# A Mamba layer on one core: low weight halves moved to VectorE, squares and first conv taps to ScalarE, group sums to PSUM, and a shorter step-size series

## The chip, the cores and the metric

The kernel runs on one core of one Trainium2 chip. The metric is the device time of one launch in microseconds (us). The engines are TensorE (PE, with its weight loads as PEld), VectorE (DVE), ScalarE (ACT), GpSimd (POOL) and SyncE (SP), which here only issues DMAs.

## The reference, cut to what matters

The whole model is two transformer-like blocks over 256 tokens of width 1024: half-step feed-forward layers, one Mamba-2 mixer, windowed attention, then a mixer of latent attention and RWKV, and a PEER layer. The change touches the Mamba-2 mixer alone:

```
zxbcdt = u @ w_in                                # 1024 -> 5152
z, xbc, dt = split(zxbcdt)                       # 2048, 3072, 32
xbc = silu(depthwise_conv(xbc, 4 taps) + b)      # xs, B, C
dt = softplus(dt + dt_bias)
y = scan(xs, dt, -exp(a_log), B, C) + d_skip * xs
y = y * silu(z)
y = rmsnorm over each of 4 groups of 512 columns
return y @ w_out                                 # 2048 -> 1024
```

With 256 tokens the scan is one chunk: `y = (C Bt * decay * dt) x`, where the decay comes from the running sum of `dt * a`.

## The kernel before, in words

Activations lie transposed: 128 features on the partitions, 256 tokens along the free dimension. Every product of float32 matrices is made of three matmuls in a faster format (`mm3`, lines 151 to 155): each operand is split into a high half, which is a rounded copy, and a low half, which is what the copy lost. Weights come from HBM in blocks of 128 x 1024 (512 KB, eight tiles of 128 x 128); `stream` (line 102) keeps one block ahead. ACT makes the high half of a block (line 93), and DVE or POOL subtracts it from the raw block for the low half (line 99). There are four raw buffers and three pairs of halves. The argument `lo_eng` says who makes the low half: "dve", "pool", or "alt", which takes turns and begins with POOL. In the Mamba layer `w_in` has 40 blocks ("alt", line 419: 20 on POOL, 20 on DVE) and `w_out` has 16 ("pool", line 463).

The layer goes through these stages. First come `dt` and the first column pairs. Then a loop of twelve column pairs (lines 450 to 456) makes B, C and xs: 48 matmuls (`proj2`), then `conv` (line 421), which scales the pair by the token's norm (line 423, DVE), multiplies the first of four taps (line 428, DVE), adds the other three (line 432, DVE, three for each of two columns) and applies silu (line 434, ACT). The tile of a column being convolved has two buffers. From pair n = 10 on, each `conv` also takes six steps of the generator `steps` (line 348). That one turns dt into the decay: a transpose, softplus, a series for its logarithm part (lines 375 to 382), then two sums over tokens by matmul with a triangle (lines 393 to 397), whose result is copied at lines 399 to 401. Line 457 runs what is left of it. Line 459 makes the first of four gate projections (`zproj`: two pairs, silu by ACT).

Then four groups run (line 548), woven with `fill`, which deals out the other three gate projections and the output projection as PE work for the gaps. A `group` (line 512) runs four `pair`s: two matmuls that spread the running sums, four Relu and one Exp on ACT (lines 477 to 479), four products on DVE (lines 483, 484), eight matmuls, two DVE operations (lines 493, 494), and POOL's square and sum (lines 496 to 500). Then the group's norm: `rs_tok` (line 184) sums the squares over the partitions by two matmuls of one column (line 190), nine short DVE operations make a reciprocal root (lines 168 to 176), two matmuls spread it (line 198), and DVE and ACT scale and split the group (lines 531 to 533) for the output projection, which adds up in four PSUM banks.

Each engine works through its own queue in order. When the program is built, a scheduler puts the instructions into these queues, near the order in which Python traces them, but an instruction that it holds ready can move ahead. A tile with one name has a fixed number of buffers; the next use waits until the last reader of the oldest is done.

Of the kernel before, what the change touches and what calls it, by code (L numbers as in the profile page):

```python
# [7 lines left out]
F32 = mybir.dt.float32  # L8
# [4 lines left out]
AF = mybir.ActivationFunctionType  # L13
OP = mybir.AluOpType
# [3 lines left out]
T = 256  # L18
KD = 8
EPS = 1e-6  # L20
# [17 lines left out]
def run(*gens):  # L38

    live = [g if isinstance(g, tuple) else (g, 1) for g in gens]  # L40
    while live:
        for x in list(live):
            for _ in range(x[1]):
                if next(x[0], live) is live:
                    live.remove(x)
                    break
# [275 lines left out]
def mamba(K, h, P, w_dt, w_in, w_out, pool):  # L322


    nc = K.nc
    V, A, TE = nc.vector, nc.scalar, nc.tensor
    ident = K.ident
    xhi, xlo, scale = K.norm_in(h, P["ssm_norm"])
# [19 lines left out]
    def steps():  # L348

        small = lambda name: pool.tile([128, 2, 32], F32, name=name)  # L350
        na = pool.tile([128, 32], F32, name="na")
        df = pool.tile([32, T], F32, name="df")
        e, s, s2 = small("sp_e"), small("sp_s"), small("sp_s2")
        A.activation(na, P["alog"], AF.Exp)
        A.activation(df, pdt[:32, :T], AF.Copy)
        yield
        ps = K.bank()
        for st in range(2):
            TE.transpose(ps[:, st * 32:(st + 1) * 32], df[:, st * 128:(st + 1) * 128], ident[:32, :32])
        yield  # L360
        for st in range(2):
            V.scalar_tensor_tensor(dtv[:, st], ps[:, st * 32:(st + 1) * 32], rt[:, st], P["dtb"], OP.mult, OP.add)
        yield
        V.scalar_tensor_tensor(e, dtv, -1.0, dtv, OP.mult, OP.min)
        A.activation(e, e, AF.Exp)
        yield
        V.tensor_scalar(s, e, 2.0, None, OP.add)
        yield
        V.reciprocal(s, s)
        yield  # L370
        V.tensor_mul(s, s, e)
        yield
        V.tensor_mul(s2, s, s)
        yield
        V.tensor_scalar(e, s2, 2.0 / 17, 2.0 / 15, OP.mult, OP.add)
        for c in (13, 11, 9, 7, 5, 3, 1):
            yield
            V.tensor_mul(e, e, s2)
            yield
            V.tensor_scalar(e, e, 2.0 / c, None, OP.add)  # L380
        yield
        V.tensor_mul(e, e, s)
        yield
        V.scalar_tensor_tensor(dtv, dtv, 0.0, e, OP.max, OP.add)
        yield
        V.scalar_tensor_tensor(s, dtv, -1.0, na.unsqueeze(1).to_broadcast([128, 2, 32]), OP.mult, OP.mult)
        yield
        ps = K.bank()
        pf = ps[:32, T:2 * T]
        for st in range(2):  # L390
            o, f = ps[:, st * 32:(st + 1) * 32], pf[:, st * 128:(st + 1) * 128]
            if st:
                TE.matmul(o, K.ones, s[:, 0], start=True, stop=False)
            TE.matmul(o, K.triu, s[:, st], start=st == 0, stop=True)
            if st:
                TE.matmul(f, s[:, 0], K.ones, start=True, stop=False)
            TE.matmul(f, s[:, st], K.triu, start=st == 0, stop=True)
        yield
        V.tensor_copy(acum, ps[:, 0:64].rearrange("p (a b) -> p a b", a=2))
        V.tensor_copy(ahl[0:32], pf)  # L400
        V.tensor_sub(ahl[32:64], pf, ahl[0:32].bitcast(F32))
# [14 lines left out]
                TE.transpose(ps[:, i * 128:(i + 1) * 128], xs[:, 4 * g + i, st * 128:(st + 1) * 128], ident)  # L416
            A.activation(xtok[:, st, g * 512:(g + 1) * 512], ps, AF.Copy)

    blk_x = K.stream(w_in, lo_eng="alt")

    def conv(n, pr):
        xp = xps[n // 2 % 2]
        V.tensor_tensor(xp[:, :, 3:], pr, rs2, OP.mult)
        w = P["convw"]
        for j in range(2):
            c = (n + j + 16) % 24
            y = pool.tile([128, T], F32, name="cv", tag="cv", bufs=2)
            V.tensor_scalar(y, xp[:, j, 0:T], w[:, c, 0:1], None, OP.mult)
            for q in range(1, 4):
                if n >= 10:  # L430
                    next(st, None)
                V.scalar_tensor_tensor(y, xp[:, j, q:q + T], w[:, c, q:q + 1], y, OP.mult, OP.add)
            dst = BC[:, n + j] if n < 8 else xs[:, n + j - 8]
            A.activation(dst, y, AF.Silu, bias=P["convb"][:, c:c + 1])

    def zproj(g):
        for m in range(2):
            o = []
            yield from K.proj2_steps(blk_x, 8 * (24 + 4 * g + 2 * m), xhi, xlo, o)
            V.tensor_tensor(zs[:, 4 * g + 2 * m:4 * g + 2 * m + 2], o[0], rs2, OP.mult)  # L440
        A.activation(zs[:, 4 * g:4 * g + 4], zs[:, 4 * g:4 * g + 4], AF.Silu)
        zdone.append(g)
# [4 lines left out]
    rs, rt = scale(lambda: up(2))  # L447
    rs2 = rs.unsqueeze(1).to_broadcast([128, 2, T])
    st = steps()
    for n in range(0, 24, 2):  # L450
        conv(n, first[n // 2] if n < 4 else K.proj2(blk_x, 8 * n, xhi, xlo))
# [2 lines left out]
                cb(g)  # L454
        if n > 12 and n % 4 == 0:
            tok((n - 16) // 4)
    run(st)
    zdone = []
    run(zproj(0))
    tok(2)  # L460
    tok(3)
    acc = [K.bank("wo") for _ in range(4)]
    blk = K.stream(w_out, lo_eng="pool")
    todo = []

    def pair(g, pr, yv, sq):

        i = g * 4 + pr
        ps = K.bank()
        sc = pool.tile([128, 2, 384], F32, name="sc", tag="sc", bufs=4)  # L470
        for e in range(2):
            hd = 2 * i + e
            TE.matmul(ps[:, e * T:(e + 1) * T], K.identr[:, hd:hd + 1].to_broadcast([64, 128]), ahl, start=True, stop=True)
        yield
        for e in range(2):
            hd = 2 * i + e
            A.activation(sc[:, e, 0:256], ps[:, e * T:e * T + 256], AF.Relu, bias=adt[:, 0, hd:hd + 1], scale=-1.0)
            A.activation(sc[:, e, 256:384], ps[:, e * T + 128:e * T + 256], AF.Relu, bias=adt[:, 1, hd:hd + 1], scale=-1.0)
        A.activation(sc, sc, AF.Exp, scale=-1.0)
        yield  # L480
        for e in range(2):
            hd = 2 * i + e
            V.scalar_tensor_tensor(sc[:, e, 0:256], sc[:, e, 0:256], adt[:, 0, 32 + hd:33 + hd], cbT[:, g, 0:256], OP.mult, OP.mult)
            V.scalar_tensor_tensor(sc[:, e, 256:384], sc[:, e, 256:384], adt[:, 1, 32 + hd:33 + hd], cbT[:, g, 256:384], OP.mult, OP.mult)
        yield
        py = K.bank()
        for e in range(2):
            hd = 2 * i + e
            o = py[64 * e:64 * e + 64]
            TE.matmul(o[:, 0:256], xtok[:, 0, hd * 64:hd * 64 + 64], sc[:, e, 0:256], start=True, stop=False)  # L490
            TE.matmul(o[:, 128:256], xtok[:, 1, hd * 64:hd * 64 + 64], sc[:, e, 256:384], start=False, stop=True)
        yield
        V.scalar_tensor_tensor(yv, xs[:, i], P["dskip"][:, i:i + 1], py[:, :T], OP.mult, OP.add)
        V.tensor_mul(yv, yv, zs[:, i])
        if pr == 0:
            nc.gpsimd.tensor_mul(sq, yv, yv)
        else:
            s1 = K.tmp.tile([128, T], F32, name="sq", tag="sq", bufs=2)
            nc.gpsimd.tensor_mul(s1, yv, yv)
            nc.gpsimd.tensor_add(sq, sq, s1)  # L500

    def w_out_blocks(g, yhi, ylo):
        for n in range(KD):
# [7 lines left out]

    def group(g):
        yv = pool.tile([128, 4, T], F32, name="yv", bufs=2, tag="yv")
        sq = pool.tile([128, T], F32, name="ysq", tag="ysq", bufs=2)
        while g not in zdone:
            yield
        yield from weave((pair(g, pr, yv[:, pr], sq) for pr in range(4)), 1)
        for _ in range(0):
            yield
        rt = K.rs_tok(sq, K.ones[:, 0:1], 1, 1.0 / 512, EPS, "n")  # L520
        for _ in range(1):
            yield
        ps = K.bank()
        for st in range(2):
            K.bcast(rt, st, 0, 128, ps[:, st * 128:(st + 1) * 128])
        yield
        yhi = pool.tile([128, 4, T], F32R, name="yhi", bufs=2, tag="yhi")
        ylo = pool.tile([128, 4, T], F32R, name="ylo", bufs=2, tag="ylo")
        for pr in range(4):
            i = g * 4 + pr  # L530
            V.scalar_tensor_tensor(yv[:, pr], yv[:, pr], P["gate"][:, i:i + 1], ps[:, :T], OP.mult, OP.mult)
            A.activation(yhi[:, pr], yv[:, pr], AF.Copy)
            V.tensor_sub(ylo[:, pr], yv[:, pr], yhi[:, pr].bitcast(F32))
            if pr % 2:
                yield
        todo.append(w_out_blocks(g, yhi, ylo))
# [1433 lines left out]
```

## Time and profile before

| | us |
|---|---|
| median of 3 runs | 2186.6 (2182.05 to 2188.41) |
| the profiled execution's own time | 2188.62 |
| its span, first to last instruction | 2186.8 |

The rows are from the profiled execution. Its time stands 2.0 above the median of the runs, and 1.8 of it lie around the span. "Busy" is the time in which an engine executes something; PE's is modelled, since matmuls overlap. PEclk is the clock that TensorE was granted, 1.00 for 2.4 GHz and 0.50 for 1.2 GHz. A line number is that of the code above.

### The profile page before, as it was taken

To read this page: it belongs to the slowest core of one execution; us is meant where nothing else is said; L and a number is where in the kernel's file an instruction comes from. 1 tells how busy PE (TensorE), PEld (TensorE's weight loads), DVE (VectorE), ACT (ScalarE), POOL (GpSimd) and SP (SyncE) were. 2 spreads that over 40 slices of the span, in tenths; PEclk is the share of its full clock that TensorE was granted. 3 is DMA by queue.
4 is the path that set the end of the run, shared out by engine and by line. 5 is a ranking of instruction groups with operands and counts; after the bars stand their busy time and mean duration, and the time that the engine had idled before them with its cause. 6 is when DMAs were issued, how large, how long until landed. Compare 5 with 4: busy or idle time off the path is not lost. (4 is left out here: it accounts for less than half of the span.)

```text
span 2186.8 us, 40880 instructions
## 1 busy us (share of the span) xinstructions
PE 2109.8 (96%) x16474; PEld 1986.3 (91%) x16474; DVE 1584.8 (72%) x2857; ACT 1055.1 (48%) x1770; POOL 407.1 (19%) x310
## 2 busy tenths in 40 slices
PE   8999898899999999999998998999999999999999
PEld 8999887799999998899997878999999998888887
DVE  7665979766567656676659678998788887555655
ACT  5444467444444445454443345553444444454454
POOL 2003335700110021100144315762000000000000
PEclk9999999999999999799998899999999999999999
DMA  6555442377555553245542205542444444555554
GB/s 218 190 185 177 136 135 101 134 191 204 185 181 184 183 184 107 102 169 188 188 164 76 80 30 194 177 151 97 157 162 155 159 160 164 189 188 191 192 188 150
DMA packets 98280, 348.14 MB, mean 159 GB/s; under 512 B 11083, under 2 KB 13996, under 8 KB 97836
## 3 DMA queue, kind: packets, MB, share of 16 engines
q1 hardware_dynamic: 98092, 345.54, 46.6%
q8 instruction: 129, 2.11, 0.4%
q14 instruction: 59, 0.48, 0.1%
HBM read 344.05 MB, written 1.44 MB: 158 GB/s over the span
## 5 line engine op out<-in xcount | busy, mean ns | idle before, releaser
L99 DVE TENSOR_TENSOR wlo<-wraw,whi 128x1024 fp32r<-128x1024 f32 x561 | 701.7, 1252 | 293.9 <-ACT whi L93 292.0
L93 ACT ACTIVATE whi<-wraw 128x1024 fp32r<-128x1024 f32 x644 | 676.5, 1053 | 394.0 <-PE ps L155 198.8
L153 PE MATMUL ps<-xhi,wlo 128*128 128x256 f32 x1960 | 562.7, 287 | 20.4 <-DVE wlo L99 9.6
L154 PE MATMUL ps<-xlo,whi 128*128 128x256 f32 x1960 | 557.3, 284 | 3.2 <-DVE xlo L182 2.6
L155 PE MATMUL ps<-xhi,whi 128*128 128x256 f32 x1960 | 554.9, 283 | 0.0
L153 PEld LDWEIGHTS ps<-xhi,wlo 128*128 128x128 f32 x1960 | 376.2, 192 | 28.8 <-DVE wlo L99 8.6
L154 PEld LDWEIGHTS ps<-xlo,whi 128*128 128x128 f32 x1960 | 376.1, 192 | 5.8 <-DVE xlo L182 5.4
L155 PEld LDWEIGHTS ps<-xhi,whi 128*128 128x128 f32 x1960 | 375.5, 192 | 0.2
L153 PE MATMUL ps<-phi,wlo 128*128 128x256 f32 x1024 | 293.9, 288 | 11.3 <-DVE wlo L99 4.6
L154 PE MATMUL ps<-plo,whi 128*128 128x256 f32 x1024 | 288.1, 281 | 0.0
L155 PE MATMUL ps<-phi,whi 128*128 128x256 f32 x1024 | 287.2, 281 | 0.0
L99 POOL TENSOR_TENSOR wlo<-wraw,whi 128x1024 fp32r<-128x1024 f32 (+1 forms) x83 | 206.8, 2495 | 167.5 <-ACT whi L93 145.5
L153 PEld LDWEIGHTS ps<-phi,wlo 128*128 128x128 f32 x1024 | 193.8, 190 | 13.1 <-DVE wlo L99 5.3
L1676 PE MATMUL pacc<-whi,cl 128*128 128x512 f32 x512 | 203.6, 398 | 1.5 <-DVE cl L1668 1.5
L1678 PE MATMUL pacc<-whi,ch 128*128 128x512 f32 x512 | 200.5, 392 | 0.0
L1677 PE MATMUL pacc<-wlo,ch 128*128 128x512 f32 x512 | 199.2, 389 | 0.0
L153 PE MATMUL ps<-ghi,wlo 128*128 128x256 f32 x704 | 197.9, 281 | 0.0
L154 PE MATMUL ps<-glo,whi 128*128 128x256 f32 x704 | 197.6, 281 | 0.0
L155 PE MATMUL ps<-ghi,whi 128*128 128x256 f32 x704 | 197.5, 280 | 0.0
L154 PEld LDWEIGHTS ps<-plo,whi 128*128 128x128 f32 x1024 | 194.0, 189 | 0.0
L155 PEld LDWEIGHTS ps<-phi,whi 128*128 128x128 f32 x1024 | 193.3, 189 | 0.0
L154 PEld LDWEIGHTS ps<-glo,whi 128*128 128x128 f32 x704 | 132.6, 188 | 0.0
(534 smaller groups left out, 3371.3 us busy)
## 6 DMA issues: line engine op xcount, KB each, us to landing
wraw<-in_w SPq DMA_DIRECT2D x262, 512.0 KB, 3.7
wraw<-in_p_u SPq DMA_DIRECT2D x128, 512.0 KB, 3.6
wraw<-in_p_v SPq DMA_DIRECT2D x128, 512.0 KB, 3.6
wraw<-in_m_win SPq DMA_DIRECT2D x40, 512.0 KB, 3.7
wraw<-in_x_win SPq DMA_DIRECT2D x20, 512.0 KB, 3.6
wraw<-in_m_wout SPq DMA_DIRECT2D x16, 512.0 KB, 3.7
wraw<-in_p_wpq SPq DMA_DIRECT2D x16, 512.0 KB, 4.3
wraw<-in_a_wq SPq DMA_DIRECT2D x8, 512.0 KB, 3.5
```

Of the source, the lines that this page charges most:

```text
L93: nc.scalar.activation(hi, w, AF.Copy)
L99: (nc.vector if lo_eng == "dve" else nc.gpsimd).tensor_sub(lo, w, hi.bitcast(F32))
L153: nc.tensor.matmul(ps, wl, xh, start=first, stop=False)
L154: nc.tensor.matmul(ps, wh, xl, start=False, stop=False)
L155: nc.tensor.matmul(ps, wh, xh, start=False, stop=last)
L1676: TE.matmul(o, cl[:, t], vh[:, f], start=False, stop=False)
L1677: TE.matmul(o, ch[:, t], vl[:, f], start=False, stop=False)
L1678: TE.matmul(o, ch[:, t], vh[:, f], start=False, stop=last)
```

## The change

- Both weight streams of the Mamba layer lose their `lo_eng`, so all 56 low halves are made by DVE: 36 move from POOL.
- The first conv tap goes from DVE to ACT (a copy with a scale from a column), 24 in all.
- The series is written with one fused operation for each term: 9 DVE operations for 16, and 21 steps of the generator for 28.
- The line that ran the rest of `steps` is gone; the first gate projection is run together with `steps`, three steps for each of its own.
- The square of each pair goes to ACT and is kept by itself: one tile of four squares (one buffer) stands for two of one sum. POOL's additions go, and `rs_tok` gets a list of four, so that PSUM adds them: eight one-column matmuls for two.

```
-        V.tensor_scalar(e, s2, 2.0 / 17, 2.0 / 15, OP.mult, OP.add)
-        for c in (13, 11, 9, 7, 5, 3, 1):
-            yield
-            V.tensor_mul(e, e, s2)
-            yield
-            V.tensor_scalar(e, e, 2.0 / c, None, OP.add)
-        yield
-        V.tensor_mul(e, e, s)
+        V.tensor_scalar(e, s2, 2.0 / 17, None, OP.mult)
+        for c in (15, 13, 11, 9, 7, 5, 3):
+            yield
+            V.scalar_tensor_tensor(e, e, 2.0 / c, s2, OP.add, OP.mult)
+        yield
+        V.scalar_tensor_tensor(e, e, 2.0, s, OP.add, OP.mult)
...
-    blk_x = K.stream(w_in, lo_eng="alt")
+    blk_x = K.stream(w_in)
...
-            V.tensor_scalar(y, xp[:, j, 0:T], w[:, c, 0:1], None, OP.mult)
+            A.activation(y, xp[:, j, 0:T], AF.Copy, scale=w[:, c, 0:1])
...
-    run(st)
     zdone = []
-    run(zproj(0))
+    run((zproj(0), 1), (st, 3))
...
-    blk = K.stream(w_out, lo_eng="pool")
+    blk = K.stream(w_out)
...
-        if pr == 0:
-            nc.gpsimd.tensor_mul(sq, yv, yv)
-        else:
-            s1 = K.tmp.tile([128, T], F32, name="sq", tag="sq", bufs=2)
-            nc.gpsimd.tensor_mul(s1, yv, yv)
-            nc.gpsimd.tensor_add(sq, sq, s1)
+        A.activation(sq[:, pr], yv, AF.Square)
...
-        sq = pool.tile([128, T], F32, name="ysq", tag="ysq", bufs=2)
+        sq = pool.tile([128, 4, T], F32, name="ysq", tag="ysq")
...
-        rt = K.rs_tok(sq, K.ones[:, 0:1], 1, 1.0 / 512, EPS, "n")
+        rt = K.rs_tok([sq[:, pr] for pr in range(4)], K.ones[:, 0:1], 1, 1.0 / 512, EPS, "n")
```

## Rows read from the trace of the kernel before

**Rows 1.** The page, part 1: busy time and share of each engine, instructions.

```profile
PE 2109.8 (96%) x16474; PEld 1986.3 (91%) x16474; DVE 1584.8 (72%) x2857; ACT 1055.1 (48%) x1770; POOL 407.1 (19%) x310
```

**Rows 2.** Busy time by stretch: conv loop, groups, and two stretches of the groups.

```profile
core 0: us, PE busy (x) PEld busy (x) DVE busy (x) ACT busy (x) POOL busy (x), PEclk, DMA share, GB/s
204.00:302.00 98.00, 88.10 (x695) 86.17 (x694) 87.82 (x166) 44.50 (x66) 34.72 (x13) 0.95 0.41 140
302.00:432.00 130.00, 117.08 (x909) 105.91 (x908) 108.30 (x186) 85.58 (x145) 79.15 (x56) 0.95 0.35 119
305.00:340.00 35.00, 35.00 (x282) 31.31 (x281) 28.13 (x43) 32.05 (x56) 17.27 (x13) 1.00 0.41 138
348.00:368.00 20.00, 20.00 (x160) 17.84 (x159) 19.94 (x34) 16.01 (x30) 12.32 (x10) 0.97 0.27 90
```

**Rows 3.** Waits of PE, 204 to 432 us: total us, times, longest.

```profile
PE ps L198 <- DVE rtn L176: 9.7, 4, 3.6
PE ps L394 <- DVE sp_s L386: 4.0, 1, 4.0
PE ps L153 <- DVE wlo L99: 3.9, 2, 2.5
PE ps L190 <- POOL ysq L500: 3.2, 2, 2.5
PE ps L153 <- POOL wlo L99: 2.0, 1, 2.0
```

**Rows 4.** DVE timeline in the conv loop: start us, us, instruction.

```profile
222.67 0.68 DVE L423 TENSOR_TENSOR xp<-ps,rs 128x512 f32<-128x512 f32 x1
223.27 2.74 DVE L428 TENSOR_SCALAR cv<-xp,pm 128x256 f32<-128x256 f32 x2
225.93 2.46 DVE L432 SCALAR_TENSOR_TENSOR cv<-xp,pm,cv 128x256 f32<-128x256 f32 x6
228.30 1.22 DVE L99 TENSOR_TENSOR wlo<-wraw,whi 128x1024 fp32r<-128x1024 f32 x1
229.44 0.61 DVE L428 TENSOR_SCALAR cv<-xp,pm 128x256 f32<-128x256 f32 x2
```

**Rows 5.** POOL timeline, the same stretch.

```profile
223.18 2.41 POOL L99 TENSOR_TENSOR wlo<-wraw,whi 128x1024 fp32r<-128x1024 f32 x1 [4.36 <-ACT whi L93]
```

**Rows 6.** Groups by line and shape, 204 to 432 us: busy us, mean ns.

```profile
L99 POOL TENSOR_TENSOR wlo<-wraw,whi 128x1024 fp32r<-128x1024 f32 x35 | 88.9, 2544 | 84.4 <-ACT whi L93 77.8 <-DVE sp_e L380 6.7
...
L483 DVE SCALAR_TENSOR_TENSOR sc<-sc,adt,cbT 128x256 f32<-128x256 f32 x32 | 30.6, 957 | 0.5 <-ACT sc L479 0.5
L99 DVE TENSOR_TENSOR wlo<-wraw,whi 128x1024 fp32r<-128x1024 f32 x20 | 26.6, 1329 | 13.8 <-ACT whi L93 13.8
...
L428 DVE TENSOR_SCALAR cv<-xp,pm 128x256 f32<-128x256 f32 x24 | 18.6, 810 | 0.2
...
L532 ACT ACTIVATE yhi<-yv 128x256 fp32r<-128x256 f32 x16 | 6.4, 416 | 16.9 <-DVE yv L531 16.9
...
L181 ACT ACTIVATE xhi<-h,gains 128x256 fp32r<-128x256 f32 x4 | 1.8, 499 | 1.6 <-DVE h L509 1.6
```

**Rows 7.** Two lines on DVE, 204 to 432 us: shortest/median/longest ns.

```profile
L428 DVE TENSOR_SCALAR cv<-xp,pm x24: 340/347/2491, 217.8 to 298.5; 128x256 f32<-128x256 f32 x24
...
L483 DVE SCALAR_TENSOR_TENSOR sc<-sc,adt,cbT x32: 470/574/2681, 314.7 to 393.0; 128x256 f32<-128x256 f32 x32
```

**Rows 8.** PE timeline, 33 matmuls, then one norm's sums, then matmuls.

```profile
205.08 0.28 PE L153 MATMUL ps<-xhi,wlo 128*128 128x256 f32 x1
...
208.97 0.50 PE L190 MATMUL ps<-ones,ssq 128*128 128x1 f32 x4
209.33 0.36 PE L153 MATMUL ps<-xhi,wlo 128*128 128x256 f32 x1
```

**Rows 9.** DVE timeline, first and last of six operations of a reciprocal root.

```profile
408.42 0.16 DVE L171 SCALAR_TENSOR_TENSOR qnt<-qna,qnt 128x2 f32<-128x2 f32 x1
...
409.40 0.16 DVE L176 SCALAR_TENSOR_TENSOR rtn<-qna,qny 128x2 f32<-128x2 f32 x1
```

## The prediction

> **What bounds the kernel now.** I read the page first: PE is busy for 96% of the span, DVE for 72%, ACT for 48%, POOL for 19% [rows 1]. That says only that matmuls carry the kernel; what the change is worth must be read where it acts. The busy time by stretch puts the Mamba layer between 204 and 432 us, 98 us of conv loop and 130 us of groups [rows 2]. In the conv loop DVE is busy for 87.8 of 98 us, in the groups for 108.3 of 130, 196.1 of 228 together. The waits of PE show what it lacks there: 9.7 us for the group's root (line 198), 4.0 for the step-size series (line 394), 3.9 and 2.0 for low halves of weights, 3.2 for POOL's squares; together 22.8 us [rows 3]. All end on DVE or POOL. Besides, PEclk is 0.95 in both stretches: 5% of 98 and of 130 us, so 4.9 and 6.5 us are lost to stretches at the lower clock, which come behind these waits. Against a stage without either, PE loses 22.8 + 11.4 = 34.2 us. That is all that a change here can win; the rest of the 228 us is PE's own work.
>
> Why DVE is late shows in the timeline. Two first taps take 2.74 us at 223.27 and 0.61 us at 229.44 [rows 4]; the long one lies under POOL's low half, 223.18 to 225.59 [rows 5]. So while POOL runs, a DVE operation can be held for some 2.1 us. The same shows in the groups: line 428 has a median of 347 ns and a mean of 810, line 483 a shortest of 470 and a mean of 957 [rows 6, 7].
>
> **The change, part by part.**
>
> *Low halves.* 36 go from POOL to DVE, 35 of them in the window [rows 6]. DVE pays one 1.22 us each [rows 4], 42.7 us. What it gets back lies between what two lines show, 24 x (810 - 347) + 32 x (957 - 470) = 11.1 + 15.6 = 26.7 us [rows 6, 7], and 35 x 2.13 = 74.6 us if each POOL operation holds DVE as at 223.27. I take the middle, 51 us. DVE's load in the window is then 196 - 51 + 43 = 188, less the taps (24 x 0.347 = 8.3) and seven series operations, on a quarter of the taps' elements (below 7 x 0.347 = 2.4; I take 1.4): 178 of some 216 us.
>
> In a conv pair DVE now needs 6.77 us from 222.67 to 229.44: scaling 0.60, two held taps 2.66, six additions 2.37, one low half 1.14, all by the next start [rows 4]. After it needs 0.60 + 2.37 + 2 x 1.22 = 5.41. PE makes 33 matmuls in 3.89 us [rows 8], 0.118 each, so 48 take 5.66 us. The loop passes from DVE to PE, by a quarter of a microsecond. Of 5.9 us of waits for low halves I leave 1.0 (bounds 0 and 5.9): pairs 10 to 14 also carry the series. **Gain 4.9.**
>
> *Series.* Nine operations for sixteen, and 21 steps for 28. `conv` asks for 6 steps in each of its last seven calls, 42 in all: the series was over before line 457, and still is. So nothing of it runs beside the gate projection: that edit does nothing. What changes is that the sums over tokens are traced in pair 16, not 18. PE's queue meets them earlier, too, and they still need DVE to be through. Of the 4.0 us wait I leave half (bounds 0 and 4.0). **Gain 2.0.**
>
> *Root of the groups.* The last six of nine operations take 1.14 us [rows 9], 0.19 each, so nine take 1.7 us when nothing holds them. Four groups would wait 6.8 us if no matmuls lay between, and 0 where `fill` covers it. With low halves queued between them on DVE I take 1.1 for each group, 4.3 for 9.7 (bounds 0 and 9.7). **Gain 5.4.**
>
> *Squares.* 28 POOL operations go, 16 on ACT come, 0.42 us each by line 532 [rows 6]; 24 taps come at 0.50 each by line 181, a copy with a scale of the same shape [rows 6]. That is 6.7 and 12 us on ACT. The wait at line 190 now ends on ACT, whose queue holds Relu, Exp and high halves: I leave 3.0 of 3.2 (bounds 0 and 6). **Gain 0.2.** The tile of squares has one buffer: the first square of a group waits until PE has summed those of the group before, and Relu and Exp of other pairs stand behind it on ACT, so PE's next products and the scaling wait too. No row shows this; bounds 0 and one wait of 2.5 us (the longest at line 190 [rows 3]) for each of three groups, 7.5; since the sums stand early in PE's queue, I take **a loss of 2.0**.
>
> *Group sums.* The four records of one sum take 0.36 us, 208.97 to 209.33 [rows 8], 0.09 each; a group goes from 4 to 16 of them, four groups add 48: **a loss of 4.3 us** of PE time (bounds 0, if they fall into waits, and 6.0, if each takes a quarter of the record's 0.50 us). The Trainium skill (VectorE: DVE Perf Modes, The TRN2 errata) gives a matmul max(60, 6 + columns) cycles of 2.4 GHz; by that, an estimate, 48 cost 1.2 us and the time would be 3.1 lower. The trace disagrees, 0.09 for 0.025 us, and I keep the row.
>
> *Clock.* With half of the waits gone I leave 6 of 11.4 us (bounds 0 and 11.4). **Gain 5.4.**
>
> The sum: -4.9 - 2.0 - 5.4 - 0.2 + 2.0 + 4.3 - 5.4 = -11.6 us. Against the profiled execution's 2188.6 that is 2177.0; it stood 2.0 above the median of the runs, so for the median I say **2175**. Moved work that I cost at nothing: taps on ACT in the conv loop, covered by ACT's idle time there (44.5 busy of 98 [rows 2]); without that cover, 12 us.
>
> **Rivals.**
>
> *ACT becomes the bound of the groups.* ACT is busy for 32.05 of 35 us from 305 to 340 and 16.0 of 20 from 348 to 368 [rows 2]; of the 6.7 us of squares some 4 fall there, so 52 of 55. For it: PE needs ACT's Exp for every pair. Against: from 368 on ACT is far less busy, over the whole 130 us it has 44 us free. Then the root's gain, that of line 190 and the groups' share of the clock (3) go: -11.6 + 5.4 + 0.2 + 3 = -3.0, and the time is about 2184, no change. The Trainium skill (ScalarE: Activation LUTs, Rules for kernel authors) says to use VectorE for a multiplication, not ScalarE; the rows agree that ACT is slower (0.50 for 0.35 us), and if that decides, this is the case.
>
> *DVE becomes the bound: slower.* If the long DVE operations are not POOL's doing, the low halves come and no stall goes: 196 + 43 - 10 = 229 us of DVE work in a stage that is 228 long. Place: the conv loop and the groups both. DVE idles 32 us now, much of it for ACT and PE; if half of that stays, the stage is 245 us, 17 longer, and the time 2204. It decides as soon as less than 17 us of stalls go. For it: the median of line 483 is above its shortest, so something small holds it often. Against: 223.18 beside 223.27 [rows 4, 5], and two lines alone hold 26.7 us.
>
> *Everything goes.* All waits and the lower clock vanish: -34.2 + 4.3 = -29.9, so 2157. For it: PE has no other wait here. Against: the root's nine operations stay in series.
>
> **How the numbers follow.** I give the forecast 0.52, ACT's rival 0.22, DVE's 0.13, everything 0.13. Two executions tell about 0.3% apart, 6.6 us: faster ends at 2180.0, slower begins at 2193.2. The forecast's own range is 2168 to 2181. The forecast (0.52, of which 0.03 falls within) and everything (0.13), with 0.03 of ACT's, give faster 0.65; the rest of ACT's and that 0.03 are the same, 0.22; DVE's is slower, 0.13. The range goes from 2160 (0.09 below it) to 2191, where nothing comes back and the group sums cost 4.3; above it lie 0.11.
>
> **What would show it.** No POOL low half between 204 and 424 us, and lines 483 and 494 near their shortest throughout. DVE busy for about 178 us in the stage, conv pairs every 5.7 us. Line 190 with 64 records for the groups, some 0.09 us apart. The sums of line 394 well ahead of the gate projection. PE's waits down from 22.8 to some 10 us, PEclk at 0.97. I am wrong if PE waits for Exp or for squares on ACT for over 8 us, if DVE's long operations stay, or if the time moves outside 204 to 444 us.

## The result, and the profile after

The median of the changed kernel is 2161.9 us (2152.1 to 2164.5, four runs), of the kernel before 2184.3 on the same chip: a ratio on record of 0.9884 with a 95% interval of 0.985 to 0.9918 (the quotient of the two medians, 0.9897, lies in it). The forecast of 2175 had the direction, but the gain is about twice as large. The time lies near the lower end of the range (2160 to 2191) and outside the forecast's own 2168 to 2181. The profiled execution took 2161.8 us, its span 2160.0.

Line numbers shift with the edit: the scaling of a conv pair is line 421, the first tap 426, the other taps 430, the products 480 and 481, the gate product 491, the squares 492, the addition to `h` 501.

First the page's busy times, to be held against [rows 1].

```profile
PE 2103.4 (97%) x16522; PEld 1981.3 (92%) x16522; DVE 1556.5 (72%) x2862; ACT 1070.0 (50%) x1810; POOL 295.3 (14%) x246
```

Only POOL's share moves by more than two points, and DVE's share is the same although it took 36 operations: something came back on DVE. The stage tells more. From the first scaling of a conv pair to the last addition to `h` it lasted 218.8 us before (216.6 to 435.4) and 193.7 after (220.1 to 413.8). That is 25.1 less, the whole gain; what lies outside moved by a few microseconds in both directions. Busy time by stretch, conv part and groups, before (columns as in [rows 2]):

```profile
216.60:302.30 85.70, 75.80 (x591) 73.87 (x589) 81.31 (x155) 38.84 (x58) 29.69 (x11) 0.94 0.40 135
302.30:435.40 133.10, 119.10 (x922) 107.56 (x921) 111.40 (x190) 87.14 (x148) 82.48 (x59) 0.95 0.35 120
```

and after:

```profile
220.10:291.00 70.90, 69.09 (x562) 67.69 (x561) 65.79 (x135) 49.29 (x82) 0.00 (x0) 0.98 0.49 157
291.00:413.80 122.80, 120.94 (x992) 110.14 (x990) 96.58 (x212) 91.81 (x164) 8.71 (x9) 1.00 0.40 130
```

DVE's busy time falls from 192.7 to 162.4 us, and PEclk rises from 0.94 and 0.95 to 0.98 and 1.00. The clock alone is worth 0.06 x 85.7 + 0.05 x 133.1 = 11.8 us before and 0.02 x 70.9 = 1.4 after. The waits of PE in the stage after (total us, times, longest), which answer to [rows 3]:

```profile
PE wo L153 <- DVE wlo L99: 1.4, 2, 0.8
PE ps L392 <- DVE sp_s L384: 0.9, 1, 0.9
PE ps L153 <- DVE wlo L99: 0.9, 2, 0.7
PE ps L154 <- DVE xlo L182: 0.4, 1, 0.4
```

These are 3.6 us; the same stage before had 23.9, the five lines of [rows 3] and 1.1 at line 154. The waits at lines 198 and 190 are gone, not shortened. So the account closes: 20.3 us of waits and 10.4 of clock won, 5.3 of group sums lost (below), together 25.4 against the 25.1 seen.

DVE's timeline in the conv loop (start, duration, engine, line, operation, tile, count), which answers to [rows 4]:

```profile
230.17 2.46 DVE L430 SCALAR_TENSOR_TENSOR cv<-xp,pm,cv 128x256 f32<-128x256 f32 x6
232.55 0.68 DVE L421 TENSOR_TENSOR xp<-ps,rs 128x512 f32<-128x512 f32 x1
233.15 2.34 DVE L99 TENSOR_TENSOR wlo<-wraw,whi 128x1024 fp32r<-128x1024 f32 x2
235.42 1.26 DVE L430 SCALAR_TENSOR_TENSOR cv<-xp,pm,cv 128x256 f32<-128x256 f32 x3
```

Nothing in it is stretched; the next scalings start at 237.79 and 243.04, a pair each 5.2 us (5.9 on the mean of the twelve, since later pairs have other work between them). The groups of DVE and ACT operations from 204 to 432 us (total, mean ns, idle before), which answer to [rows 6]:

```profile
L99 DVE TENSOR_TENSOR wlo<-wraw,whi 128x1024 fp32r<-128x1024 f32 x63 | 77.0, 1226 | 26.1 <-ACT whi L93 26.0
L480 DVE SCALAR_TENSOR_TENSOR sc<-sc,adt,cbT 128x256 f32<-128x256 f32 x32 | 15.3, 479 | 0.9 <-ACT sc L476 0.9
L491 DVE TENSOR_TENSOR yv<-yv,zs 128x256 f32<-128x256 f32 x16 | 6.7, 419 | 0.0
L426 ACT ACTIVATE cv<-xp,pm 128x256 f32<-128x256 f32 x24 | 10.8, 499 | 2.1 <-DVE xp L421 1.7
L492 ACT ACTIVATE ysq<-yv 128x256 f32<-128x256 f32 x16 | 6.6, 416 | 6.4 <-DVE yv L491 2.1 <-DVE qnt L171 1.8 <-DVE qny L172 1.8
```

Line 480 (483 before) has a mean of 479 ns where it had 957, and DVE waits for ACT's products for 0.9 us in all. Last the group sums in PE's timeline:

```profile
352.40 0.28 PE L155 MATMUL wo<-yhi,whi 128*128 128x256 f32 x1
352.52 1.84 PE L190 MATMUL ps<-ones,ysq 128*128 128x1 f32 x16
354.29 0.66 PE L487 MATMUL ps<-sc,xtok 128*64 128x256 f32 x4
```

From 352.52 to the next matmul at 354.29 there are 1.77 us for 16 records, 0.111 each; 48 more records cost 5.3 us.

### The profile page after: what moved, and what is told of

It reads as the page before. It is cut to its first block, busy times and chain, and to the rows that moved or that the text cites. A ratio compares the mean times of both kernels' runs of the same rounds, so it can differ in the third digit from the quotient of the medians.

```text
span 2160.0 us, 40955 instructions
## 1 busy us (share of the span) xinstructions
PE 2103.4 (97%) x16522; PEld 1981.3 (92%) x16522; DVE 1556.5 (72%) x2862; ACT 1070.0 (50%) x1810; POOL 295.3 (14%) x246
## 3 DMA queue, kind: packets, MB, share of 16 engines
q8 instruction: 130, 2.13, 0.4%
## 5 line engine op out<-in xcount | busy, mean ns | idle before, releaser
L99 DVE TENSOR_TENSOR wlo<-wraw,whi 128x1024 fp32r<-128x1024 f32 x597 | 743.0, 1246 | 304.6 <-ACT whi L93 302.5
L153 PEld LDWEIGHTS ps<-phi,wlo 128*128 128x128 f32 x1024 | 194.6, 190 | 11.8 <-ACT phi L1489 4.3
L153 PEld LDWEIGHTS ps<-ghi,wlo 128*128 128x128 f32 x704 | 132.4, 188 | 0.0
```

Of the source, the lines that this page charges most:

```text
L99: (nc.vector if lo_eng == "dve" else nc.gpsimd).tensor_sub(lo, w, hi.bitcast(F32))
L153: nc.tensor.matmul(ps, wl, xh, start=first, stop=False)
```

## The experiments

Theory A: POOL's low halves hold DVE's operations, and moving them to DVE ends the holds, which is most of the gain. Against it stands that the other parts carry it, or that DVE becomes the bound. Ratios are to the kernel before, with their 95% interval. For comparison, a kernel that differs from the changed one only in running the series and the first gate projection one after the other, with the same instructions in the same order on every engine, was run again later: 0.9882 [0.985, 0.9913], where 24 to 26 us below the kernel before were expected.

**Only the low halves** (kernel before, with this alone):

```
-    blk_x = K.stream(w_in, lo_eng="alt")
+    blk_x = K.stream(w_in)
...
-    blk = K.stream(w_out, lo_eng="pool")
+    blk = K.stream(w_out)
```

> The kernel before with one edit: all low halves of the Mamba layer by DVE. Theory A (while POOL works, it holds DVE; taking 36 POOL subtractions away sets DVE free): the Mamba layer, from the first scaling of a pair to the last addition to h, goes from 218.8 us to 200 us or less, and the time falls by 15 to 20 us, most of the change's 25. Theory B (POOL's low halves come late themselves, and PE waits for those): only the 2.0 us that PE waited for POOL's low halves go, with some 2 us of lower clock behind them; the time falls by 2 to 4 us and DVE's long operations stay.

Measured: 2166.3 us, 0.9909 [0.9876, 0.9941], the stage 198.8 us: 20 of the 25 us. The waits of PE in the stage, line numbers as before:

```profile
PE ps L153 <- DVE wlo L99: 4.9, 4, 1.9
PE wo L153 <- DVE wlo L99: 3.3, 2, 2.8
PE ps L394 <- DVE sp_s L386: 2.0, 1, 2.0
PE ps L190 <- POOL ysq L500: 1.7, 2, 0.9
PE ps L198 <- DVE rtn L176: 0.9, 1, 0.9
```

The root's wait falls from 9.7 to 0.9 us and that of line 190 from 3.2 to 1.7 without any edit to the squares. The longer of the two waits at line 190 before, 2.5 us, was DVE's: POOL's last square had waited for the gate product. Before the shorter, 0.7 us, the square stood behind a low half in POOL's own queue (399.51 to 402.10). What is left are low halves, with taps and 16 series operations still on DVE.

**All but the low halves** (changed kernel, with `lo_eng="alt"` and `"pool"` again).

> The kernel after, with the 36 low halves back on POOL (squares and taps on ACT, shorter series, sums in PSUM stay). Theory A: DVE's long operations come back in the low halves' shadow; 5 to 10 us of the 25 are kept, the time is some 15 to 20 us above the kernel after. Theory B: the squares and the series were what made PE wait, so 20 us or more are kept.

Measured: 2179.0 us, 0.9993 [0.9964, 1.0022], the stage 211.4 us. On the whole run these parts bring nothing that can be told: the interval spans 1, though the median lies 7 us below that of the kernel before and the profiled stage is 7 us shorter. Theory B's 20 us are refuted; Theory A's 5 to 10 us kept are neither shown nor excluded. The holds are back, as on the gate product (shortest, median, longest ns, first and last start):

```profile
L491 DVE TENSOR_TENSOR yv<-yv,zs x16: 408/424/2559, 313.4 to 395.5; 128x256 f32<-128x256 f32 x16
```

**POOL's low halves made again, and read by nobody** (changed kernel; output unchanged, `spare` is only written):

```
+            if lo_eng == "pool2" or self.flip2:
+                nc.gpsimd.tensor_sub(self.spare, w, hi.bitcast(F32))
```

> The kernel after, and POOL makes its former 36 low halves once more into a tile that nobody reads. PE waits for none of them. Theory A: DVE is held again, lines 480 and 491 reach 2 us and more, the Mamba layer grows by 10 us or more and the time with it. Theory B: nothing waits for POOL, so the time is that of the kernel after within 3 us.

Measured: 2210.3 us, 1.0112 [1.0044, 1.018], slower than before, the stage 241.6 us. Nobody waits for these results, so the loss comes from POOL being busy. A small part goes by another way than DVE: POOL still reads the raw block and the high half when ACT wants their buffers, and ACT waits 8.0 us for that, in three waits. The main part shows on DVE, which has the same work as in the changed kernel and is busy for 222.4 us in the stage where it was 162.4. The stage, then the timelines of DVE and POOL in the conv loop:

```profile
220.00:461.60 241.60, 205.71 (x1551) 190.13 (x1550) 222.42 (x347) 140.73 (x245) 105.56 (x42) 0.92 0.35 114
...
225.71 0.68 DVE L427 TENSOR_TENSOR xp<-ps,rs 128x512 f32<-128x512 f32 x1
226.31 4.59 DVE L436 SCALAR_TENSOR_TENSOR cv<-xp,pm,cv 128x256 f32<-128x256 f32 x6
...
227.09 2.74 POOL L99 TENSOR_TENSOR spare<-wraw,whi 128x1024 fp32r<-128x1024 f32 x1 [4.69 <-ACT whi L93]
```

Six taps that took 2.46 us take 4.59 beside one POOL operation, 2.13 more: the size of the hold at 223.27 [rows 4]. The other reading is which lines are held:

```profile
L427 DVE TENSOR_TENSOR xp<-ps,rs x12: 674/682/693, 220.0 to 303.5; 128x512 f32<-128x512 f32 x12
L436 DVE SCALAR_TENSOR_TENSOR cv<-xp,pm,cv x72: 463/474/2641, 221.4 to 309.3; 128x256 f32<-128x256 f32 x72
```

The scaling, which reads PSUM, is never longer than 693 ns, although six of the twelve overlap a copy; the taps, which read two SBUF tiles, reach 2641. The two lines that Theory A had named, 480 and 491 (486 and 497 here), were not held (487 and 424 ns at most): they hardly met a copy. The taps, the low halves of weights and those of the scaled groups were held instead. The Trainium skill (SBUF — State Buffer, Who interferes with whom) says that a VectorE instruction with two SBUF inputs and a GpSimd instruction that reads SBUF shut each other out for a whole instruction, and one with at most one SBUF input, outside the two-port modes, does not. These rows agree. The first taps of the kernel before, which read one SBUF tile and a column, were held too, up to 2491 ns [rows 7]; whether they ran in a two-port mode no row shows. Theory A is shown from both sides: the low halves alone bring most of the gain, and the POOL work alone, without its use, takes all of it away and more.

**The series edit and the first gate projection** (changed kernel, `run(st); run(zproj(0))` for the combined line).

> The kernel after, with the line that runs the series beside the first gate projection put back to one after the other. By the count of steps (42 asked for in the conv loop, 21 there) the series is over before that line. Theory: the edit does nothing, the order on every engine is that of the kernel after, and the time is that of the kernel after, 25 us below the kernel before, within 3 us. Rival: the series does run beside the projection; then the wait for its sums grows by 2 us or more.

Measured: 2162.0 us, 0.989 [0.9861, 0.9919]; the instructions stand in the same order on every engine. That edit does nothing, as predicted.

**The old series** (changed kernel, with 16 operations again).

> The kernel after, with the series as it was, 16 DVE operations in 28 steps. Theory G (the longer series delays its sums): PE's wait at the sums over tokens goes from 0.9 to 3 us or more, and the time is 2 to 4 us above the kernel after. Theory H (the series has slack without POOL's holds): the wait stays near 1 us, the time within 2 us.

Measured: 2153.9 us, 0.9866 [0.982, 0.9911]. The wait for the sums is 2.0 us where the changed kernel has 0.9, between the two theories, yet the time is no longer; the median is even 8 us lower, with overlapping intervals. Theory G's longer time is not borne out: the fused series wins a microsecond of wait that cannot be seen in the whole.

**First taps on DVE** (changed kernel).

```
-            A.activation(y, xp[:, j, 0:T], AF.Copy, scale=w[:, c, 0:1])
+            V.tensor_scalar(y, xp[:, j, 0:T], w[:, c, 0:1], None, OP.mult)
```

> The kernel after, with the first conv taps back on DVE. Theory E (the conv loop is DVE's by a narrow margin): DVE needs 6.0 us for a pair where PE needs 5.7, so 4 to 6 us more than the kernel after, and PE waits for low halves in the loop. Theory F (DVE has the room, ACT's taps only add a hop): within 2 us.

Measured: 2158.4 us, 0.9883 [0.9836, 0.993]. PE's waits for low halves grow from 2.3 to 7.3 us, as Theory E said, the stage from 193.7 to 196.4; the time is the same, as Theory F said. With 5 us more of waits the stage is 2.7 us longer, which is below what two executions can tell.

**Squares on POOL** (changed kernel, with the sum of squares on POOL and two buffers, as before).

> The kernel after, with the squares and their additions back on POOL (16 records at line 190). PE is spared 48 x 0.11 = 5.3 us. Theory A: 28 POOL operations of 0.7 us hold DVE in the groups, PE's waits at lines 190 and 198 come back in part, so the time is equal to the kernel after, from 3 us less to 5 us more. Theory B (what POOL holds is of no weight): 4 to 6 us less than the kernel after.

Measured: 2160.1 us, 0.9884 [0.9838, 0.9929], the stage 192.0 us. PE waits 1.7 us for POOL's squares and 1.0 for the root, and the 48 sums are not paid: it comes out even, as Theory A allowed. Neither way is shown to be better.

**Each group sum twice** (changed kernel; the list is doubled and the mean's factor halved, so the output stays).

```
-        rt = K.rs_tok([sq[:, pr] for pr in range(4)], K.ones[:, 0:1], 1, 1.0 / 512, EPS, "n")
+        rt = K.rs_tok([sq[:, pr] for pr in range(4)] * 2, K.ones[:, 0:1], 1, 1.0 / 1024, EPS, "n")
```

> The kernel after, with every group's sum of squares made twice over and halved by the factor behind it: 128 records at line 190 for 64. Theory C (the one-column matmuls lie on PE's own path, since PE no longer waits in the groups): 64 x 0.11 us, as the trace of the kernel after spaces them, so 7 us more than the kernel after. Theory D (they fall into time in which PE has nothing else): within 2 us of the kernel after.

Measured: 2172.3 us, 0.9941 [0.9913, 0.9968], the stage 207.5 us. PE's timeline, then its stretches (length, busy, PEclk, DMA):

```profile
328.36 3.63 PE L190 MATMUL ps<-ones,ysq 128*128 128x1 f32 x32
331.92 0.66 PE L487 MATMUL ps<-sc,xtok 128*64 128x256 f32 x4
...
328.00:332.00 4.00, 4.00 (x39) 1.00 0.41 131
332.00:336.00 4.00, 4.00 (x24) 0.69 0.35 111
336.00:340.00 4.00, 4.00 (x32) 0.88 0.06 25
```

Each sum still costs 0.111 us, so 64 more cost 7.1, as Theory C said; by the medians the loss is some 10 us. The profiled execution is the slowest of twelve (2179.2 us); its groups took 136.8 us where they took 122.8, 14 more. The rest is the granted clock: 0.69 behind this run of sums, and 0.60, 0.67 and 0.50 behind the other three, while PE shows no idle time; over the groups it is 0.94, so some 8 us. In the changed kernel's profile the runs of 16 sums do not do this:

```profile
332.00:336.00 4.00, 4.00 (x35) 1.00 0.39 131
```

But that is not a rule for 16. In the profile of the second kernel of the next experiment the first run of 16 ends at 327.9, up to there every engine has the instructions of the changed kernel in the same order, and the clock falls all the same:

```profile
328.00:332.00 4.00, 4.00 (x23) 0.63 0.39 117
```

Behind the first run of 16 in the kernel with all but the low halves it is 0.69, too.

**DVE's room in the groups.** To double DVE's load of low halves in the groups, 16 of `w_out` are made twice (one into an unread tile), the unread one first, then, in a second kernel, last:

```
+        if twice:
+            nc.vector.tensor_sub(self.spare, w, hi.bitcast(F32))
```

> The kernel after, and DVE makes the 16 low halves of w_out twice, the second time into a tile that nobody reads: 16 x 1.22 = 19.5 us more of DVE's own work in the groups, where it is busy for 97 of 123 us. Theory K (in the groups PE has 27 to 42 matmuls between the sums and the spreading of the root, which cover a root that only queues, and it was the holds of 2 us each in the middle of a root that broke the cover): at most 4 us more than the kernel after, PE's waits for the root stay below 2 us. Theory L (DVE's load as such sets the waits, whoever makes it): 8 us more or more, and PE's waits at line 198 come back with 4 us or more.

> As the run before with the 16 low halves of w_out made twice by DVE, but the needed one first and the unread one behind it, so that no low half comes later for it. Theory K (roots that only queue are covered by PE's matmuls between; only holds broke that): within 3 us of the kernel after, PE's waits at line 198 below 2 us. Theory L (DVE's load as such sets the waits): 6 us more or more, waits for roots of 4 us or more. Theory M (what cost 6 us was the needed low half behind the spare one): the waits for low halves fall from 7.8 us to 4 or less and the time with them.

Measured: 2167.3 us, 0.9913 [0.9887, 0.9939], and 2178.5 us, 0.9944 [0.9914, 0.9975]. The first is confounded, since the half that PE needs then stands behind the spare one; its loss of some 6 us lies between the two theories, and its wait for the root, 1.0 us, is as Theory K said. In the second the needed half stands first, and yet more is lost. Its waits of PE from 291 to 431 us:

```profile
PE ps L157 <- DVE wlo L101: 4.5, 1, 4.5
PE ps L194 <- ACT ysq L497: 2.6, 2, 1.5
PE wo L157 <- ACT yhi L529: 1.9, 2, 1.5
PE ps L202 <- DVE rtn L180: 1.0, 1, 1.0
```

The 16 spare halves are 19.9 us of DVE time. PE waits 11.3 us in the groups where it waited 1.8, and part of it shows as waits for ACT, which itself waited for DVE. The loss is over the 6 us of Theory L, but it does not take the path that L gave: the root waits 1.0 us, not 4. Nor do the low-half waits fall to Theory M's 4; they are 6.3 us in the whole stage. In the first kernel's profile PE waits 7.9 us in the groups. So in both profiles DVE, busy for 97 of 123 us there in the changed kernel, did not take 20 us more without PE waiting. What that costs is not settled: the second kernel's profile is of one of its slowest executions (2181.1 us), its granted clock in the groups is 0.92, which is 11 us of the loss and begins to fall before the first spare half (348.7), and three of its twelve executions took 2156.9 to 2165.2 us, about as long as the changed kernel. Why the second order costs more than the first was not settled either.

**The same edit elsewhere.** The low halves that POOL makes in the mixers between 904 and 1327 us, in the layer behind it, or in both, go to DVE (`lo_eng` dropped there).

> The kernel after, with the low halves of the mixers alone moved to DVE. Theory A there: 3 to 8 us less than the kernel after. Rival: DVE has other work in the mixers that PE waits for, and low halves queue before it: 2 us more or more.

> The kernel after, with the low halves of the PEER layer alone moved to DVE. DVE is busy there for 162 of 170 us, so it is DVE that bounds it. Theory A there: if each of about 27 holds costs 2 us and the work 1.22, 5 to 15 us less than the kernel after. Rival: the holds are shorter there than the work moved, and the time grows by as much as DVE's load, 5 us or more.

> The kernel after, with all other low halves that POOL makes, 47 in the mixers and the PEER layer, by DVE as well. Theory A applied there: each POOL low half holds DVE for about 2 us and costs DVE 1.22 itself, DVE is busy for 320 of the 378 us, so 5 to 15 us less than the kernel after. Rival (there POOL works in DVE's idle time): 5 us more or more.

Measured: mixers 2157.4 us, 0.9856 [0.9834, 0.9878]; the layer behind 2171.4 us, 0.9923 [0.99, 0.9946]; both 2165.5 us, 0.9897 [0.9877, 0.9917]. For the mixers that would be within Theory A's 3 to 8 us, but the interval overlaps that of the changed kernel; for both together Theory A's 5 to 15 us less did not come. In the layer behind it the change turns against itself. Busy time from 1301 to 1492 us, and PE's first wait in it:

```profile
1301.00:1492.00 191.00, 170.99 (x1357) 167.34 (x1357) 181.82 (x537) 97.04 (x166) 50.46 (x50) 0.96 0.48 160
...
PE ps L153 <- DVE wlo L99: 15.4, 8, 4.3
```

against the changed kernel's

```profile
1301.00:1482.00 181.00, 167.85 (x1347) 163.80 (x1347) 169.91 (x511) 97.75 (x166) 114.72 (x76) 0.97 0.49 166
...
PE ps L153 <- DVE wlo L99: 3.2, 2, 2.3
```

DVE was busy for 94% there already; about 27 low halves of POOL moved there, 33 us of work at 1.22 each, and DVE is busy for 11.9 us more, so only some 21 us of holds came back. The stretch gets 10 us longer. This is the rival in which DVE becomes the bound, in a place that has no room.

**Mixers on DVE and squares on POOL together.**

> The kernel after, with the low halves of the mixers by DVE and the Mamba layer's squares back on POOL (so 48 one-column matmuls fewer). If the two parts add up as each did alone: 4 to 6 us less than the kernel after. Rival: the two gains were within the spread of the runs, and the time is that of the kernel after within 3 us.

Measured: 2159.2 us, 0.9885 [0.9851, 0.9918]. The gains do not add up, as the rival said. The mixers' edit alone has the lowest ratio of all, but its interval overlaps that of the changed kernel; no version is shown to beat it.

## Why the prediction was right or wrong

**Right.** The cause and its place. POOL's operations hold DVE for some 2.1 us, the low halves bring DVE more than they cost, and the gain lies in the Mamba stage. DVE's returned holds: 192.7 + 33 x 1.22 - 9.7 - 162.4 = 60.9 us, where I took 51 between 26.7 and 74.6 (33 low halves of POOL lay in this stage; 9.7 are the prediction's figures for the taps and series operations). Summed from the traces, what DVE's operations took above the shortest of their line falls from 63.2 to 3.3 us, nearly the same. DVE's load fell by 30 us (192.7 to 162.4), where I had 18 (196 to 178, in the wider window of [rows 2]). The edit to the first gate projection does nothing. The taps on ACT cost nothing that can be seen. Each step's direction was right, but for the loss at the one-buffer tile, which is nil. Two readings were off, without weight: line 428 lies in the conv loop and not in the groups [rows 7], and in the pairs that start 5.2 us apart a matmul takes 0.109 us, where the row of 33 gave 0.118 and pairs every 5.7.

**Wrong: the residues.** Each wait was left a part by judgement, where nearly nothing stayed. By terms:

- *Low halves*: 1.0 us left, 2.3 measured. The one that I left too small.
- *Series*: 2.0 left, 0.9 measured; with the low halves alone it is 2.0, so the fused operations took the other 1.1.
- *Root*: 4.3 left, 0 measured. The step that failed is "with low halves queued between them on DVE I take 1.1 for each group". Between the sums and the spreading stand 27 to 42 matmul rows in the changed kernel, some 3 to 5 us at 0.118 each. Before there were 33 to 38 in three groups, which waited 2.6, 2.7 and 0.9 us all the same, and 14 in the last, which waited 3.6: with the holds in it the chain was longer than the cover. I had the 1.7 us of nine unheld operations and named `fill`, but did not count that cover. The root's chain, from its first operation to its last, shrank from 20.8 us over four groups to 13.5. So operations do queue between, as I said, but all of it lies under matmuls.
- *Line 190*: 3.0 left, 0 measured. I took the wait to move to ACT. Its longer part, 2.5 us, was DVE's lateness passed on by POOL; the low halves alone leave 1.7, and these come back when the squares go back to POOL, so the move to ACT is worth 1.7 here.
- *One tile of squares*: a loss of 2.0, none measured: PE waits for no square in the stage after.
- *Group sums*: a loss of 4.3, 5.3 measured, 0.111 each for 0.09. The 0.025 us that the prediction worked out, as an estimate, from the Trainium skill (VectorE: DVE Perf Modes, The TRN2 errata) is not borne out; each of these records has a weight load of its own.
- *Clock*: 6 left of 11.4, 1.4 of 11.8 measured. The step "with half of the waits gone I leave 6" scaled the loss with the sum of the waits. But a wait costs clock only where a stretch at 1.2 GHz follows it, and behind the remaining waits, of 0.9 us at most, I find one such stretch, behind line 392 (264 to 268 us, PEclk 0.64). This term rests on one profiled execution of each kernel.

With the measured terms the sum is -3.6 - 3.1 - 9.7 - 3.2 - 0.7 (line 154, 1.1 to 0.4, which I left out) + 5.3 - 10.4 = -25.4 us. Three terms carry the difference of 13.8 to my -11.6: the root 4.3, the clock 5.0 and line 190 with the squares' tile 5.0; the small ones nearly cancel.

**Rivals.** "Everything goes" was the nearest (2157, a chance of 0.13). Its argument against, that the root's nine operations stay in series, is true and did not matter, since they are covered. ACT as the bound of the groups is not borne out: it is busy for 91.8 of 122.8 us, and PE does not wait for it in them. DVE as the bound is refuted for this stage, and seen where low halves were put on a DVE busy for 94%.

## What to carry to other kernels

Before costing a move off POOL, look whether the long outliers of DVE's operations lie under POOL's: then POOL's time is paid on DVE too, and the move can pay with DVE already the busiest. Whether what is left of a wait stays is a matter of cover: hold the rows that the waiting engine has queued between the cause and the wait against the length of the chain that they have to cover. The same move in a stretch where DVE is busy for 94% loses, so it is decided stage by stage.

## What the runs showed that I had not expected

- Behind each run of 26 to 32 one-column matmuls the granted clock falls (0.50 to 0.69 in the next four microseconds) although PE shows no idle time. Behind 1.8 us runs of 16 it stays at 1.00 in the changed kernel's profile, but not always: the same instructions gave 0.63 in another execution. What decides between them no run here separates.
- The scalings, which read PSUM, are not held: of 24 in the kernel before and the one with spare copies, 15 overlap a POOL operation and none is longer than 693 ns, where operations with two SBUF inputs reach 2641.
- Executions of one program differ by more than some of the effects here, and the granted clock goes with it: with the spare halves last, from 2156.9 us at a mean clock of 0.988 to 2182.0 at 0.973.
